# One Trainium2 core, a two-layer block with attention, convolution and linear attention: taps and low parts of weights get tied places in VectorE's queue

## The chip, the core and the metric

The kernel runs on one core of one Trainium2 chip. Its engines work beside each other, each through its own queue in the order in which the program was written to it: TensorE (PE) multiplies matrices, VectorE (DVE), ScalarE (ACT) and GpSimd (POOL) work on tiles, SyncE (SP) starts DMAs. An instruction at the head of a queue that waits for another engine holds up all that stand behind it. Times are device microseconds (us); the measured time of a kernel is the median of several runs.

## The reference

A token stream of 1024 channels goes through two layers of a first block and two more of a second. Each layer of the first block has a mixer with three branches over the same normalised and modulated input: attention with 8 heads (2 for keys and values) and rotary positions, gated linear attention (GLA), and a convolution. The convolution is the part that matters here:

```
glu   = a * sigmoid(g)                       # 1024 channels, from two projections of 1024 columns
conv  = depthwise_conv(glu, w_dw, width 31)  # 31 taps per channel, along the tokens
u     = layernorm(conv) * gain + bias
out_c = silu(u) @ w_conv_o                   # 1024 x 1024
f     = sum over branches of gate_b * (branch_b @ w_b)
```

All of it is in fp32. After the mixer comes a gated feed-forward network.

## The kernel before

**Products in three parts.** An fp32 product is computed as three products of rounded parts. A weight tile of 128 columns and 1024 rows (`raw`, 1 MB by DMA for two tiles) is split by `wsplit` (line 354 and on): ScalarE rounds it to the high part (`whi`, line 362), DVE subtracts to get the low part (`wlo`, listed under line 288, as every two-input operation is). For each of the eight blocks of 128 rows `mm_fm` (lines 386 to 388) then issues hi x hi, hi x lo and lo x hi, 24 matmuls in all; for keys, values and queries (lines 467 to 469) weights and data change sides. There are two `raw` buffers, three of `whi`, three of `wlo`, and three PSUM buffers `pm` for the results, which ScalarE or DVE must empty before they are used again.

**Two mixers.** In the first layer a mixer works on 512 tokens (512 columns per matmul), in the second on 256. The first takes the time from about 60 to 600 us, the second from about 1200 to 1700 us.

**Convolution.** `conv` computes 30 taps per channel tile on DVE as scalar_tensor_tensor instructions, acc = glu * w + acc, and the middle one with the bias on ScalarE. It does two channel tiles at a time (`ca_10457` and `ca_10458` are the first two of the second mixer, `ca_10463` and `ca_10464` the last); after a pair, GpSimd adds it to the channel sum `cs`. `conv_taps` loads the tap weights (`cwr`), transposes them on TensorE (line 1310) and copies them out as `cw`. `conv_norm` multiplies the finished sum by a constant matrix (`ones_d`, line 1346) to spread the mean over the partitions, subtracts it, squares, sums the squares (`csq`, `onesk`, line 1366), takes the rstd on GpSimd, scales and splits the result in parts for the product with `w_conv_o`.

**What sets the order.** The Python program is a set of generators, called lanes. Projections go along the main line, and at every projected tile `tick` lets each lane advance by its rate: the lane "conv" by CRATE0 = 1.3 steps in the first mixer and CRATE1 = 1.0 in the second, where a step is two taps of two channel tiles, so four DVE instructions. `merge` projects the gates (`mt`, a tanh on ScalarE) of a branch and its output product; before the latter, `flush` runs the lanes that the branch needs to their end. A scheduler then puts the recorded instructions into the queues by priority, with times of its own; taps carry priority 600 (CP), `wsplit` a more urgent one (WP = -100). `issue_after` gives it an extra edge: the instruction may not stand ahead of the one named. On one and the same engine that needs no semaphore.

Of the kernel before, what the change touches and what calls it, by code (L numbers as in the profile page):

```python
# [9 lines left out]
F32 = mybir.dt.float32  # L10
# [3 lines left out]
ALU = mybir.AluOpType  # L14
# [8 lines left out]
          "g": 5664, "gate": 6688}  # L23
WP = -100
CRATE0 = 1.3
CRATE1 = 1.0
ARATE0 = 0.6
ARATE1 = 0.6
GRATE0 = 0.8
GRATE1 = 0.6  # L30
CP = 600
PLO0A = 0
PLO0B = 0
PLO0 = PLO0A, PLO0B
PLO1A = 0
# [136 lines left out]
class Act:  # L172
    def __init__(self, hi, lo, hp=None, lp=None):
        self.hi, self.lo, self.hp, self.lp = hi, lo, hp, lp
# [13 lines left out]
class Builder:  # L188
    NU = 71

    def __init__(self, ctx, tc, ins, out, dbg=None, stop=None):
        self.tc, self.nc, self.I, self.out = tc, tc.nc, ins, out
        self.dbg, self.stop = dbg, stop
        self.n = 0
        self.lanes = {}
        self.pool_lo = 0
        self.nsplit = 0
        self.wpri = WP
        self.behind = None
        self.fheld = None  # L200
        self.spare = {}
        self.lo_behind = []
        self.hook = self.lo_after = None
        self.ns = [None]
        P = lambda **k: ctx.enter_context(tc.tile_pool(**k))
        self.cp = P(name="cp", bufs=1)
        self.sp = P(name="sp", bufs=12)
        self.up = P(name="up", bufs=self.NU)
        self.wp = P(name="wp", bufs=2)
        self.rp = P(name="rp", bufs=2)  # L210
        self.hp = P(name="hp", bufs=3)
        self.lp = P(name="lp", bufs=3)
        self.pm = P(name="pm", bufs=3, space=PSUM)
        self.ps = P(name="ps", bufs=5, space=PSUM)
# [63 lines left out]
        for _ in gen:  # L278
            pass

    def flush(self, *lanes):
        ls = [self.lanes[k] for k in lanes if k in self.lanes]
        while any(l[0] for l in ls):
            for l in ls:
                self.step(l)

    def tt(self, out, a, b, op, eng=None):
        return (eng or self.nc.vector).tensor_tensor(out=out, in0=a, in1=b, op=op)  # L288
# [68 lines left out]
    def wsplit(self, src, shape, pri=None):  # L357
        hi = self.hp.tile(list(shape), F32R, tag="whi", name=self.nm("whi"))
        lo = self.lp.tile(list(shape), F32R, tag="wlo", name=self.nm("wlo"))
        self.nsplit += 1  # L360
        with self.pri(self.wpri if pri is None else pri):
            self.nc.scalar.copy(hi, src)  # L362
            on_pool = self.pool_lo and self.nsplit % self.pool_lo == 0
            after = self.lo_behind.pop() if self.lo_behind else None
            with self.tc.issue_after(after.ins) if after else nullcontext():
                self.tt(lo, src, hi.bitcast(F32), ALU.subtract, self.nc.gpsimd if on_pool else None)
        return hi, lo

    def fm(self, w, c0, ncols, nk=8):
# [945 lines left out]
    def conv(self, l, cts, glu, acc, csum, cw, ns):  # L1315

        v = lambda x: x.rearrange("p (s t) -> p s t", s=ns)
        with self.pri(CP):
            for c in cts:
                self.act(acc[c], glu[c], AF.Identity, scale=cw[:, c, 15:16], bias=self.vt0[:, 8 * l + c : 8 * l + c + 1])  # L1320
        n = 0
        for k in range(31):
            d = k - 15
            if d == 0:
                continue
            lo, hi = max(0, -d), 256 - max(0, d)
            with self.pri(CP):
                for c in cts:
                    a = v(acc[c])[:, :, lo:hi]
                    self.stt(a, v(glu[c])[:, :, lo + d : hi + d], cw[:, c, k : k + 1], a, ALU.mult, ALU.add)  # L1330
            n += 1
            if n == 30:
                with self.pri(CP):
                    if cts[0] == 0:
                        self.tt(csum, acc[0], acc[1], ALU.add, self.nc.gpsimd)
                    else:
                        for c in cts:
                            self.tt(csum, csum, acc[c], ALU.add, self.nc.gpsimd)
            if n % 2 == 0:
                yield  # L1340
# [126 lines left out]
    def mixer(self, l, a, xs, start):  # L1467
# [9 lines left out]
        glu, acc = [], [self.u((128, T), F32, "ca") for _ in range(8)]  # L1477
# [9 lines left out]
        for m in range(0, 8, 2):  # L1487
# [13 lines left out]
            if m == 0:  # L1501
                cw = self.conv_taps(l)
            self.bg("conv", [self.conv(l, (m, m + 1), glu, acc, csum, cw, len(xs))], (CRATE0, CRATE1)[l])
        self.run(ai), self.run(gi)
        self.flush("mod")
        self.rope_tabs(l)
        kn, v = {}, {s: [self.u((128, 2, 256), F32R, n) for n in ("vh", "vl")] for s in both}
# [50 lines left out]
        def merge(bi, wname, oact, pre=0, lanes=(), then=None):  # L1558

            gi = self.proj_fm(w, IN_OFF["gate"] + bi * D, D, ar, T)  # L1560
            gts = []

            def gate():
                t = self.uh(T, "mt")
                self.act(t, next(gi), AF.Tanh, scale=0.5)
                gts.append(t)

            for _ in range(pre):
                gate()
            self.flush(*lanes)  # L1570
            if callable(oact):
                oact = oact()
            if then:
                then()
            yi = self.proj_fm(I[wname][l], 0, D, oact, T)
            for m in range(8):
                if m >= pre and m % 2 == 0:
                    gate(), gate()
                t, py = gts[m], next(yi)
                self.stt(t, t, 1.0, py, ALU.add, ALU.mult)  # L1580
                if macc[m] is None:
                    macc[m] = t
                else:
                    self.tt(macc[m], macc[m], t, ALU.add, nc.gpsimd if MP >> (2 * l + bi % 2) & 1 else None)
            self.run(gi), self.run(yi)
# [12 lines left out]
        if VG[l]:  # L1598
            vproj()
        merge(0, "w_att_o", oatt, PRE0[l], ("heads", "att"), None if GLE[l] else logs)  # L1600
        oatt = kT = qT = None
        self.flush("gla", "conv")

        self.pool_lo = (PLO0, PLO1)[l][1]
        ocv = self.act_alloc(8, T)
# [2 lines left out]
        self.bg("gla", [self.gla_scores(xs, kg, qg, A)], (GRATE0, GRATE1)[l] * len(xs))  # L1608
        acc = glu = csum = None
        merge(2, "w_conv_o", ocv, PRE2[l], ("conv",))  # L1610
        ocv = None
        if not VG[l]:
# [71 lines left out]
        elif PH1:  # L1684
            self.bg("pre", [self.prehold([(I["w_out"][l], 0, 512, 512)], PW1)])
        merge(1, "w_gla_o", gated, PRE1[l], ("gla",))
        rs = rp = on = og = kg = qg = vg = A = None
        self.B = self.st = None
# [491 lines left out]
```

## Time and profile before

| | |
|---|---|
| median of 3 runs | 2551.83 us (2550.2 to 2553.7) |
| the profiled execution | 2553.78 us, its span 2551.9 us |
| mean granted clock of TensorE | 0.98 |
| PE busy | 2418.1 us, 95% of the span |
| DVE busy | 1624.0 us, 64% |
| ACT busy | 1180.8 us, 46% |
| POOL busy | 518.1 us, 20% |
| DMA | 345.41 MB, 135 GB/s |

Busy times are shares of the whole span; what an engine is worth in a stretch is read from that stretch alone. The matmuls of 256 columns start 0.12 us apart at full clock, those of 512 columns 0.23 us. In the lists of waits and the timelines a bracket holds the idle time of the engine ahead of an instruction, and what ended it.

### The profile page before, as it was taken

What the parts mean: (1) busy time and instruction counts of PE and PEld (TensorE: products, weight loads), DVE (VectorE), ACT (ScalarE), POOL (GpSimd) and SP (SyncE); (2) the same over time, 40 slices, a digit from 0 to 9 for tenths busy, and PEclk for the clock granted to TensorE, in tenths of its full rate; (3) what the DMA queues carried; (4) which work ended last, traced back from release to release, by engine and by line L of the source; (5) the groups of instructions that cost most, each with busy time, mean ns of one, the idle gap of its engine ahead of it and who ended that gap; (6) DMA issues with size and microseconds to landing.
All of it is one profiled execution on the core that took longest, in us unless ns stands there. A gap on an engine that the chain in (4) does not pass through costs nothing. (4 is left out here: it accounts for less than half of the span.)

```text
span 2551.9 us, 38718 instructions
## 1 busy us (share of the span) xinstructions
PE 2418.1 (95%) x15227; PEld 2079.3 (81%) x15227; DVE 1624.0 (64%) x2700; ACT 1180.8 (46%) x2225; POOL 518.1 (20%) x460
## 2 busy tenths in 40 slices
PE   7989999899999999999899997998999999999998
PEld 5767887688877777776879897888987899888997
DVE  5878997884365443343799687766625656556564
ACT  3224567654343322232445855653443644446443
POOL 1002003791014000003310006531062100112001
PEclk9999999999999999999999998999999999999999
DMA  8432203223433444355233242642664246643454
GB/s 254 150 129 78 83 21 99 67 84 108 140 100 132 143 158 162 116 187 189 73 124 100 85 150 84 198 149 87 218 206 134 92 157 211 199 145 106 155 192 149
DMA packets 277690, 345.41 MB, mean 135 GB/s; under 512 B 12894, under 2 KB 208888, under 8 KB 277508
## 3 DMA queue, kind: packets, MB, share of 16 engines
q1 hardware_dynamic: 277508, 342.94, 41.7%
q8 instruction: 120, 1.97, 0.3%
q14 instruction: 62, 0.51, 0.1%
HBM read 341.85 MB, written 1.05 MB: 134 GB/s over the span
## 5 line engine op out<-in xcount | busy, mean ns | idle before, releaser
L386 PE MATMUL pm<-hi,whi 128*128 128x256 f32 (+1 forms) x2824 | 918.6, 327 | 23.5 <-ACT mt L298 13.1
L387 PE MATMUL pm<-lo,whi 128*128 128x256 f32 (+1 forms) x2824 | 911.4, 323 | 3.5 <-POOL lo L288 2.0
L388 PE MATMUL pm<-hi,wlo 128*128 128x256 f32 (+1 forms) x2824 | 909.5, 323 | 5.2 <-DVE wlo L288 5.1
L362 ACT CAST whi<-raw 128x1024 fp32r<-128x1024 f32 (+1 forms) x464 | 484.1, 1048 | 838.1 <-PE pm L387 506.2
L288 DVE TENSOR_TENSOR wlo<-raw,whi 128x1024 fp32r<-128x1024 f32 (+2 forms) x437 | 551.6, 1265 | 410.6 <-ACT whi L362 409.2
L386 PEld LDWEIGHTS pm<-hi,whi 128*128 128x128 f32 x2824 | 541.2, 192 | 68.2 <-ACT mt L298 13.9
L387 PEld LDWEIGHTS pm<-lo,whi 128*128 128x128 f32 x2824 | 542.7, 192 | 50.5 <-issue 7.4
L388 PEld LDWEIGHTS pm<-hi,wlo 128*128 128x128 f32 x2824 | 541.8, 192 | 46.5 <-DVE wlo L288 7.2
L291 DVE SCALAR_TENSOR_TENSOR ca<-gt,cw,ca 128x242 f32<-128x242 f32 (+28 forms) x480 | 267.6, 607 | 0.2
L468 PE MATMUL pm<-wlo,hi 128*128 128x512 f32 x536 | 211.8, 395 | 9.3 <-DVE wlo L288 7.1
L467 PE MATMUL pm<-whi,hi 128*128 128x512 f32 x536 | 213.4, 398 | 5.5 <-DVE qn L288 5.5
L469 PE MATMUL pm<-whi,lo 128*128 128x512 f32 x536 | 211.0, 394 | 0.0
L288 POOL TENSOR_TENSOR s<-s,mhalf 128x1 f32<-128x1 f32 (+2 forms) x82 | 67.0, 816 | 483.7 <-DVE s L295 445.1
L288 POOL TENSOR_TENSOR hl<-hr,hh 128x512 fp32r<-128x512 f32 (+1 forms) x38 | 56.6, 1492 | 472.7 <-ACT hh L454 416.9
L468 PEld LDWEIGHTS pm<-wlo,hi 128*128 128x128 f32 x536 | 101.9, 190 | 32.5 <-DVE wlo L288 7.5
L467 PEld LDWEIGHTS pm<-whi,hi 128*128 128x128 f32 x536 | 101.9, 190 | 29.1 <-issue 4.7
L469 PEld LDWEIGHTS pm<-whi,lo 128*128 128x128 f32 x536 | 101.6, 190 | 21.4
L288 POOL TENSOR_TENSOR eq<-B 128x256 f32<-128x256 f32 x96 | 91.3, 971 | 51.0 <-DVE ptot L291 27.7
L288 POOL TENSOR_TENSOR ek<-B 128x256 f32<-128x256 f32 (+1 forms) x100 | 100.1, 1020 | 1.1 <-DVE mt L288 0.6
L288 POOL TENSOR_TENSOR wlo<-raw,whi 128x1024 fp32r<-128x1024 f32 (+1 forms) x35 | 80.6, 2316 | 95.2 <-ACT whi L362 89.8
L467 PE MATMUL pm<-hh,hi 128*128 128x512 f32 (+2 forms) x258 | 92.6, 362 | 4.9 <-ACT hh L432 2.5
L468 PE MATMUL pm<-hl,hi 128*128 128x512 f32 (+2 forms) x258 | 93.0, 362 | 1.3 <-POOL hl L288 1.0
(327 smaller groups left out, 3362.3 us busy)
## 6 DMA issues: line engine op xcount, KB each, us to landing
raw<-in_w_in_dram SPq DMA_DIRECT2D x84, 1024.0 KB
aw<-in_w_ada_dram SPq DMA_DIRECT2D x192, 256.0 KB
raw<-in_w_gate_up_dram SPq DMA_DIRECT2D x40, 1024.0 KB
raw<-in_w_ff_gate_dram SPq DMA_DIRECT2D x21, 1024.0 KB
raw<-in_w_ff_up_dram SPq DMA_DIRECT2D x21, 1024.0 KB
raw<-in_w_down_dram SPq DMA_DIRECT2D x20, 1024.0 KB
raw<-in_w_ff_down_dram SPq DMA_DIRECT2D x18, 1024.0 KB
raw<-in_w_att_o_dram SPq DMA_DIRECT2D x8, 1024.0 KB
```

The lines of the kernel that those rows point to most:

```text
L288: return (eng or self.nc.vector).tensor_tensor(out=out, in0=a, in1=b, op=op)
L291: return self.nc.vector.scalar_tensor_tensor(out=out, in0=a, scalar=s, in1=b, op0=op0, op1=op1)
L362: self.nc.scalar.copy(hi, src)
L386: mm(out, lhsT=hi[:, k, :], rhs=a.hi[k], start=(first and k == 0), stop=False)
L387: mm(out, lhsT=hi[:, k, :], rhs=a.lo[k], start=False, stop=False)
L388: mm(out, lhsT=lo[:, k, :], rhs=a.hi[k], start=False, stop=(last and k == nk - 1))
L467: f(p, lhsT=a.hi[kk][:, sl], rhs=hi, start=first, stop=False)
L468: f(p, lhsT=a.hi[kk][:, sl], rhs=lo, start=False, stop=False)
L469: return f(p, lhsT=a.lo[kk][:, sl], rhs=hi, start=False, stop=last)
```

## The change

The lane "conv" advances by 1.2 steps per tile in the second mixer. Each conv step leaves its last tap in a list (`taps`), and `wsplit` remembers the last low part that DVE makes (`last_lo`). A low part is then ordered behind the third last step recorded (CLAG = 3), and every tap behind the last low part recorded. In the first `merge` of a mixer, `flush` advances the lane "conv" by two steps per round beside the attention lanes. After the flush of "gla" and "conv" the list is emptied. The number of instructions on PE, DVE, POOL and SP is the same as before. In the rows of order below, line numbers after the change are 10 to 16 higher for the same line of code.

```diff
-CRATE1 = 1.0
+CRATE1 = 1.2
+FRATE = 2.0
+CLAG = 3
...
-    def flush(self, *lanes):
+    def flush(self, *lanes, along=None, rate=1.0):
+
         ls = [self.lanes[k] for k in lanes if k in self.lanes]
+        al, n = self.lanes.get(along), 0.0
         while any(l[0] for l in ls):
             for l in ls:
                 self.step(l)
+            n += rate
+            while al and n >= 1.0:
+                n -= 1.0
+                self.step(al)
...
             after = self.lo_behind.pop() if self.lo_behind else None
+            if len(self.taps) >= CLAG:
+                after = self.taps[-CLAG]
             with self.tc.issue_after(after.ins) if after else nullcontext():
-                self.tt(lo, src, hi.bitcast(F32), ALU.subtract, self.nc.gpsimd if on_pool else None)
+                i = self.tt(lo, src, hi.bitcast(F32), ALU.subtract, self.nc.gpsimd if on_pool else None)
+                if not on_pool:
+                    self.last_lo = i
...
-            with self.pri(CP):
+            with self.pri(CP), self.tc.issue_after(self.last_lo.ins) if self.last_lo else nullcontext():
                 for c in cts:
                     a = v(acc[c])[:, :, lo:hi]
-                    self.stt(a, v(glu[c])[:, :, lo + d : hi + d], cw[:, c, k : k + 1], a, ALU.mult, ALU.add)
+                    i = self.stt(a, v(glu[c])[:, :, lo + d : hi + d], cw[:, c, k : k + 1], a, ALU.mult, ALU.add)
             n += 1
+            if n % 2 == 0:
+                self.taps.append(i)
...
-            self.flush(*lanes)
+            self.flush(*lanes, along="conv" if bi == 0 else None, rate=FRATE)
...
         self.flush("gla", "conv")
+        self.taps = []
```

On DVE in the first mixer, between the first and the second pair of channel tiles (`ca_127` and `ca_128`, then `ca_129` and `ca_130`): `wlo_1268` is the low part of the first K/V weight tile, `adar_1225` the sum of modulation and bias that needs eight matmuls of TensorE and a copy on ScalarE. Before:

```order
151 L291 SCALAR_TENSOR_TENSOR ca_128<-gt_661,cw_677,ca_128 128x2x241
152 L288 TENSOR_TENSOR wlo_1268<-raw_1265,whi_1267 128x1024
153 L288 TENSOR_TENSOR wlo_1300<-raw_1265,whi_1299 128x1024
154 L291 SCALAR_TENSOR_TENSOR gt_1152<-gt_1152,ga_1041 128x512
155 L295 TENSOR_SCALAR modT<-ps_1192 128x8
156 L288 TENSOR_TENSOR wlo_1334<-raw_1331,whi_1333 128x1024
157 L291 SCALAR_TENSOR_TENSOR gt_1189<-gt_1189,ga_1078 128x512
158 L288 TENSOR_TENSOR adar_1225<-adar_1225,ab_1198 4x512
159 L291 SCALAR_TENSOR_TENSOR ca_129<-gt_818,cw_677,ca_129 128x2x241
160 L291 SCALAR_TENSOR_TENSOR ca_130<-gt_858,cw_677,ca_130 128x2x241
```

After:

```order
154 L301 SCALAR_TENSOR_TENSOR gt_1189<-gt_1189,ga_1078 128x512
155 L305 TENSOR_SCALAR modT<-ps_1463 128x8
156 L298 TENSOR_TENSOR adar_1225<-adar_1225,ab_1198 4x512
157 L301 SCALAR_TENSOR_TENSOR ca_129<-gt_818,cw_677,ca_129 128x2x241
158 L301 SCALAR_TENSOR_TENSOR ca_130<-gt_858,cw_677,ca_130 128x2x241
159 L301 SCALAR_TENSOR_TENSOR ca_129<-gt_818,cw_677,ca_129 128x2x242
160 L301 SCALAR_TENSOR_TENSOR ca_130<-gt_858,cw_677,ca_130 128x2x242
161 L298 TENSOR_TENSOR wlo_1268<-raw_1265,whi_1267 128x1024
```

The low part, which stood six rows ahead of the modulation's sum, now stands behind it and behind the first four taps of the next pair. On TensorE the modulation's eight matmuls moved ahead of the K/V tile's, and on SP their weight loads ahead of a `raw` load.

On DVE at the start of the second mixer, where the tap weights are copied out (`cw_10624`), `gt` is the glu that the taps read and `wlo_10727` and `wlo_10785` are the low parts of the next two gate and value tiles. Before:

```order
1184 L288 TENSOR_TENSOR wlo_10727<-raw_10724,whi_10726 128x1024
1185 L288 TENSOR_TENSOR wlo_10785<-raw_10724,whi_10784 128x1024
1186 L291 SCALAR_TENSOR_TENSOR gt_10608<-gt_10608,ga_10499 128x256
1187 L691 BN_AGGR mv_10673<-bn_10670 128x2
1188 L295 TENSOR_SCALAR s_10675<-mv_10673 128x1
1189 L291 SCALAR_TENSOR_TENSOR s_10681<-mv_10673,s_10677 128x1
1190 L288 TENSOR_TENSOR wlo_10843<-raw_10840,whi_10842 128x1024
1191 L295 TENSOR_SCALAR cw_10624<-ps_10615 128x248
1192 L288 TENSOR_TENSOR wlo_10880<-raw_10840,whi_10879 128x1024
```

After:

```order
1187 L301 SCALAR_TENSOR_TENSOR gt_10608<-gt_10608,ga_10499 128x256
1188 L305 TENSOR_SCALAR cw_10624<-ps_10615 128x248
1189 L301 SCALAR_TENSOR_TENSOR ca_10457<-gt_10561,cw_10624,ca_10457 128x241
1190 L301 SCALAR_TENSOR_TENSOR ca_10457<-gt_10561,cw_10624,ca_10457 128x242
1191 L301 SCALAR_TENSOR_TENSOR ca_10458<-gt_10608,cw_10624,ca_10458 128x241
1192 L301 SCALAR_TENSOR_TENSOR ca_10457<-gt_10561,cw_10624,ca_10457 128x243
1193 L301 SCALAR_TENSOR_TENSOR ca_10458<-gt_10608,cw_10624,ca_10458 128x242
1194 L298 TENSOR_TENSOR wlo_10727<-raw_10724,whi_10726 128x1024
1195 L301 SCALAR_TENSOR_TENSOR ca_10458<-gt_10608,cw_10624,ca_10458 128x243
1196 L301 SCALAR_TENSOR_TENSOR ca_10457<-gt_10561,cw_10624,ca_10457 128x244
1197 L301 SCALAR_TENSOR_TENSOR ca_10458<-gt_10608,cw_10624,ca_10458 128x244
1198 L298 TENSOR_TENSOR wlo_10785<-raw_10724,whi_10784 128x1024
```

The two low parts stood ahead of the copy of the tap weights; now they stand behind it and behind five and eight taps of the first pair.

On TensorE at the end of the second mixer's convolution, `ps_13658` is the product of the channel sum `cs` with `ones_d`, and `pm` are gate tiles of the convolution's branch. Before:

```order
7027 L388 MATMUL pm_13871<-hi_10007,wlo_13868 128x256
7028 L386 MATMUL pm_13871<-hi_10008,whi_13867 128x256
7029 L387 MATMUL pm_13871<-lo_10012,whi_13867 128x256
7030 L1346 MATMUL ps_13658<-cs_10465,ones_d 128x256
7031 L388 MATMUL pm_13871<-hi_10008,wlo_13868 128x256
7032 L386 MATMUL pm_13871<-hi_10008,whi_13867 128x256
```

After:

```order
6947 L400 MATMUL pm_13632<-hi_10010,whi_13628 128x256
6948 L401 MATMUL pm_13632<-lo_10014,whi_13628 128x256
6949 L402 MATMUL pm_13632<-hi_10010,wlo_13629 128x256
6950 L1362 MATMUL ps_13658<-cs_10465,ones_d 128x256
6951 L400 MATMUL pm_13686<-hi_10007,whi_13682 128x256
6952 L401 MATMUL pm_13686<-lo_10011,whi_13682 128x256
6953 L402 MATMUL pm_13686<-hi_10007,wlo_13683 128x256
```

The product stood eight matmuls into the tile `pm_13871`; now it stands three tiles and these eight matmuls earlier, right behind `pm_13632`. On DVE the last taps of `ca_10463` and `ca_10464` moved with it, from ahead of `wlo_13973`, which is for a tile behind `pm_13871`, to ahead of `wlo_13434`, twelve low parts earlier.

## Rows read from the trace of the kernel before

**Rows 1.** The page, busy time, share of the span and instructions of each engine
```profile
PE 2418.1 (95%) x15227; PEld 2079.3 (81%) x15227; DVE 1624.0 (64%) x2700; ACT 1180.8 (46%) x2225; POOL 518.1 (20%) x460
```
**Rows 2.** Stretches: length, busy PE, PEld, DVE, ACT, POOL, clock, DMA share, GB/s
```profile
130.00:200.00 70.00, 60.67 (x273) 46.88 (x272) 51.47 (x93) 21.27 (x68) 7.26 (x6) 0.90 0.38 128
...
1250.00:1310.00 60.00, 55.03 (x363) 51.23 (x362) 52.27 (x103) 30.52 (x51) 12.61 (x11) 0.91 0.48 149
...
1440.00:1500.00 60.00, 58.01 (x389) 53.30 (x389) 37.72 (x75) 51.41 (x72) 0.00 (x0) 1.00 0.33 103
...
1520.00:1567.00 47.00, 31.82 (x203) 30.68 (x202) 39.13 (x68) 25.75 (x57) 22.18 (x26) 0.78 0.36 112
```
**Rows 3.** Waits of PE, 1500 to 1570 us: total us, times, longest
```profile
PE pm L386 <- ACT mt L298: 12.0, 2, 6.7
PE ps L1346 <- POOL cs L288: 3.2, 1, 3.2
```
**Rows 4.** Timeline of PE, 1519 to 1567: start, us, instruction, [idle before <- releaser]
```profile
1519.91 0.28 PE L386 MATMUL pm<-hi,whi 128*128 128x256 f32 x1
...
1532.89 1.22 PE L1346 MATMUL ps<-cs,ones_d 128*128 128x256 f32 x2 [3.23 <-POOL cs L288]
...
1534.13 0.41 PE L386 MATMUL pm<-hi,whi 128*128 128x256 f32 x1
1534.34 0.41 PE L387 MATMUL pm<-lo,whi 128*128 128x256 f32 x1
...
1543.94 1.28 PE L1366 MATMUL ps<-onesk,csq 128*128 128x1 f32 x5
...
1566.43 0.41 PE L386 MATMUL pm<-hi,whi 128*128 128x256 f32 x1
```
**Rows 5.** Timeline of POOL, the end of the channel sum
```profile
1531.24 1.60 POOL L288 TENSOR_TENSOR cs<-cs,ca 128x256 f32<-128x256 f32 x2 [105.73 <-DVE ca L291]
```
**Rows 6.** Timeline of ACT, the mt of the second stop
```profile
1560.72 0.36 ACT L298 ACTIVATE mt<-pm 128x256 f32<-128x256 f32 x1
```
**Rows 7.** Timeline of DVE, 1440 to 1500 us, low parts and taps
```profile
1461.78 1.23 DVE L288 TENSOR_TENSOR wlo<-raw,whi 128x1024 fp32r<-128x1024 f32 x1 [5.25 <-ACT whi L362]
...
1487.21 0.97 DVE L291 SCALAR_TENSOR_TENSOR ca<-gt,cw,ca 128x241 f32<-128x241 f32 x2
...
1496.03 2.01 DVE L291 SCALAR_TENSOR_TENSOR ca<-gt,cw,ca 128x246 f32<-128x246 f32 x5
```
**Rows 8.** Timeline of PE in the first mixer, 133 to 190 us
```profile
133.11 0.40 PE L468 MATMUL pm<-wlo,hi 128*128 128x512 f32 x1
...
188.52 0.80 PE L468 MATMUL pm<-wlo,hi 128*128 128x512 f32 x1 [7.12 <-DVE wlo L288]
189.11 0.63 PE L469 MATMUL pm<-whi,lo 128*128 128x512 f32 x1
189.54 0.63 PE L467 MATMUL pm<-whi,hi 128*128 128x512 f32 x1
```
**Rows 9.** Timeline of DVE in the first mixer, 122 to 180 us
```profile
122.16 2.12 DVE L288 TENSOR_TENSOR wlo<-raw,whi 128x1024 fp32r<-128x1024 f32 x1 [0.49 <-ACT whi L362]
...
145.46 0.68 DVE L288 TENSOR_TENSOR adar<-adar,ab 4x512 f32<-4x512 f32 x1 [10.59 <-ACT adar L638]
...
179.41 6.02 DVE L291 SCALAR_TENSOR_TENSOR ca<-gt,cw,ca 128x508 f32<-128x508 f32 x9
```
**Rows 10.** Waits of PE, 125 to 250 us
```profile
PE ps L915 <- DVE ra L288: 3.2, 1, 3.2
```
**Rows 11.** Timelines of PE and DVE at the start of the second mixer
```profile
1256.64 0.40 PE L1310 MATMUL ps<-cst,cwr 31*128 31x31 f32 x4 [1.59 <-DMA cwr<-in_conv_w_dw_dram]
...
1259.42 0.58 PE L1310 MATMUL ps<-cst,cwr 31*128 31x31 f32 x4 [1.53 <-DMA cwr<-in_conv_w_dw_dram]
...
1263.54 0.58 PE L386 MATMUL pm<-hi,whi 128*128 128x256 f32 x1 [1.53 <-ACT ga L1491]
...
1260.03 0.42 DVE L295 TENSOR_SCALAR cw<-ps 128x248 f32<-128x248 f32 x1 [3.40 <-PE ps L1310]
```

More of the change, by code (lines that the diff above doesn't have):

```diff
@@ L202, in __init__ @@
         self.lo_behind = []
+        self.last_lo = None
+        self.taps = []
         self.hook = self.lo_after = None
@@ L1602, in mixer @@
         self.flush("gla", "conv")
+        self.taps = []
         self.pool_lo = (PLO0, PLO1)[l][1]
```

## The prediction

> **What bounds the kernel now.** I read the page's busy times first. TensorE is busy for 2418 of 2552 us [rows 1], so a change of order can gain only from its 134 us of gaps and from the stretches in which its clock is halved, and can lose wherever it makes TensorE wait. Next I cut the first block's two mixers into stretches [rows 2]. Almost all of TensorE's loss in them lies in three: 130 to 200 us (60.7 us busy of 70, clock 0.90), 1250 to 1310 (55.0 of 60, clock 0.91) and 1520 to 1567 (31.8 of 47, clock 0.78). In the last one the list of waits has three entries that matter, 12.0 us in two waits for ScalarE's mt and 3.2 us for GpSimd's cs [rows 3]. The timelines of the single engines then say why.
>
> **The end of the second mixer's convolution.** The reader is to follow one chain. DVE has little to do ahead of 1487 us: before the low part at 1461.8 it stands still for 5.3 us until ScalarE has made the high part [rows 7], and in 1440 to 1500 it is busy for 37.7 of 60 us [rows 2]. Only at 1487.2 does it begin the taps of the last pair of channel tiles (ca_10463 and ca_10464 in the order) [rows 7]. So GpSimd's channel sum waits until 1531.2 for those taps [rows 5], and TensorE, which has the ones_d product of that sum in its queue, stops at 1529.7 until 1532.9 [rows 3, 4]. Then the chain of the normalisation (subtract, square, sum, rstd, scale, split) runs with hardly any matmuls left to stand beside it: TensorE stops for 6.7 and for 5.3 us more [rows 3], both times for a PSUM buffer that ScalarE has not yet emptied, since its mt, at 1560.7 the second time [rows 6], stands in ScalarE's queue behind pieces of this chain.
>
> **The change part by part.** No operation is added or taken away; what moves is order, and with the low parts the release of weight buffers. The 240 taps of a layer cost what they did: 0.40 us each in the second mixer (five in 2.01 us) beside 1.2 us for a low part [rows 7].
>
> First, the end of the second mixer. With 1.2 steps per tile and the two kinds of DVE work tied together, the last pair's taps stand between the low parts of the tiles of 1455 to 1500. 60 taps of 0.40 us are 24 us. Some 18 of them were in that stretch already (1487 to 1500), the other 42 need 17 us, and DVE had 22.3 us free there [rows 2]. So they should end about 1500 instead of 1531, with each low part some 2 to 3 us ahead of its first matmul; I price this at 0 to +2 us and take 0. What this gives is in the order of TensorE: ones_d now stands one matmul after the eighth gate tile, ahead of the matmul that starts at 1519.9 [rows 4], and the sum it needs is then 20 us old. From there to the second tile after the chain (1566.4) the kernel takes 46.5 us [rows 4]. In it are seven tiles of 24 matmuls at 0.12 us, 20.2 us, and some 2 us of small ones; 24 us are waits and half clock. In the new order the chain starts 13 us earlier and has 61 tile matmuls (7.3 us) between ones_d and the sums of squares, where it takes 11.0 us now (1532.9 to 1543.9, [rows 4]): about 3 us of wait remain there. From the sums to the mt that holds up the next-to-last tile it takes 16.8 us now (1543.9 to 1560.7, [rows 4, 6]), against 12 us of tile and small matmuls: 3.5 us of wait, and about 2 more at the rstd and at the split parts. With 4 us of half clock that is 12.5 of the 24, so 12 us are saved. Bounds: 18 us if the clock stays up and the chain is shorter in emptier queues, 6 us if the waits add up as they stand now.
>
> After such a stop the rows show matmuls of 256 columns 0.21 us apart instead of 0.12: 1534.1 and on, after a wait of 3.2 us [rows 4]. Of 512 columns they go at 0.43 instead of 0.23 after the wait of 7.1 [rows 8], a granted clock at the lower of two levels, 1.2 instead of 2.4 GHz. The Trainium skill (TensorE: Matmul & The Clock Gate, Part 1: The HAM clock gate) says that the slow state is the default and that activity releases it, and so speaks against a change that turns three long stops into four short ones. If by that rule each of the four cost a half-clock stretch like the one after 1532.9, the gain here would fall to about 9 us; if none did, it would be near 16. No row of this stretch shows four such stops in a row.
>
> Second, the first mixer, 130 to 200 us. Taken away is the longest wait there: TensorE stands from 181.4 to 188.5 for a low part that DVE computes only after eleven taps and an add, and then runs 14 matmuls at half clock, 14 x 0.20 = 2.8 us [rows 8, 9]. Now DVE has that low part every four taps, and its sum of durations puts it at about 185, when TensorE, late by the next paragraph, comes for it. So some 10 us go.
>
> Added is a wait at 133 us. There TensorE's first K/V matmul with a low part starts at 133.1 [rows 8], on a low part that DVE made from 122.2 to 124.3, ready with 9 us to spare [rows 9]. In the new order this one (wlo_1268) stands behind the add of adar and four taps of the next pair, and the adar behind eight matmuls of the modulation, which TensorE now does before the K/V tiles. In the rows of before the adar add starts at 145.5 after 10.6 us idle [rows 9]. Moved up with its matmuls, it can start at about 134.5; four taps of 0.64 and the low part of 1.2 bring the low part to 138 to 141, and TensorE to a stop of 4 to 6 us, with 2 us of half clock. Behind it on DVE stand the next low parts and the K norms, so that the wait for the first qn at 160 grows by about 1. Together 5 + 2 + 1 = +8, and −10 + 8 = −2. In 220 to 245 DVE is then further ahead with its taps than before, and the wait for ra there (3.2 us [rows 10]) may shrink: I take −1 more, in all −3, between −9 (the new stop is 2 us and that wait goes too) and +6 (the new stop is 10 us and the old one only moves).
>
> Third, the start of the second mixer, 1250 to 1310 us. TensorE's eight transposes of the tap weights (cwr) wait for their DMA at 1256.6 and 1259.4 in either order [rows 11]. Now they stand before 22 matmuls that before filled the time around them, and wlo_10727 stands behind the weights' copy and five taps, so those matmuls can't start until the copy at 1260.0 [rows 11], two first terms on ScalarE (1 us), five taps (2.0) and the low part (1.2): about 1264.4. The 44 matmuls of two tiles, the first half of them at half clock, take 22 x 0.21 + 22 x 0.12 = 7.3 us and end near 1271.7. In the order of before, 24 of them and 9 transposes are left at 1263.5, after the last of three stops [rows 11]: 33 x 0.21 = 6.9 us, 1270.4. That is +1. For the next 40 us DVE needs 1.2 + 4 to 6 x 0.40 = 2.8 to 3.6 us per weight tile and TensorE 24 x 0.12 = 2.9, so TensorE is pushed back by up to 2 us, most of which later stops give back, where TensorE waits for norms that DVE makes no later than before. I take +1.5; from −2 to +20 (a rival, below).
>
> The remaining places I cost at nothing: ahead of 130 us in the first mixer four to eight taps (2.6 to 5 us) now stand before each low part, and the cover is a lead like the 9 us above; where it is gone, a low part that is late costs the duration of a tap or two, 0.6 to 1.3 us. In the later parts the same DVE work fits between the same matmuls.
>
> **The sum.** −12 − 3 + 1.5 = −13.5 us. The profiled execution took 2553.8 us (span 2551.9 and 1.9 around it), 2 us above the median of 2551.8. On the median this gives 2538 us.
>
> **The rivals.**
> The first: DVE becomes the bound of the second mixer's first stretch. For it speaks that DVE is already busy for 52.3 of the 60 us after 1250 [rows 2]. If it has six taps at every one of the next 20 tiles, it falls behind TensorE by 3.6 − 2.9 = 0.7 us at each, 14 us, and with half clock after the stops 20 us. It decides once the lag is over 15 us, because then the gains of the other two places are eaten: 2553.8 + 20 − 12 − 3 is 2559, on the median 2557. Against it: the order has four taps between most low parts, not six, and in the attention part much of DVE's work waits for TensorE and ScalarE and not the reverse.
> The second: the end of the convolution is early but the chain stays as long as it is, because ScalarE and GpSimd work through the gated linear attention's pieces in the same queues; the waits for mt stay at two thirds. Then 6 of the 12 us come: 2544.
> The third: ties hold DVE back more than forecast in the first mixer (+6 instead of −3) and the end brings 8: 2551.8 − 8 + 6 + 1.5 = 2551, no change that can be seen.
> The fourth: all the stops shrink, −18 − 7 − 1 = −26: 2526.
>
> **How the numbers follow.** Forecast and its neighbourhood (2532 to 2542): 0.40. Second rival: 0.20. Fourth: 0.13. Third: 0.13. First: 0.14. A difference of 0.2% (5.1 us) is about what a measurement of this kernel can tell from none. Faster by more is the forecast, the second and the fourth, less a little of the second's edge: 0.71. Same: 0.14. Slower: 0.15. The range 2527 to 2556 leaves out the outer half of the fourth and of the first. The likeliest case's own range is 2532 to 2544.
>
> **What would show it.** Right: the ones_d product runs at 1510 to 1525 without a wait, and no wait for mt there is over 4 us; the stretch corresponding to 1520 to 1567 takes some 34 us; the wait at 181 is gone and one of 4 to 6 us stands near 135; in 1250 to 1265 TensorE stops about 10 us in all. Wrong: low parts named as what TensorE waits for over 1264 to 1345 or 1480 to 1500 with more than 5 us in all, or a stop for mt of 5 us or more beside a ones_d product that was on time.

## The result, and the profile after

The changed kernel takes 2567.9 us (median of 4 runs, 2564.7 to 2571.5) against 2552.5 us before in the same sessions: ratio 1.0062, 95% interval 1.0044 to 1.0079. It is 15 us slower, where 14 us faster was forecast. The profiled execution took 2568.5 us, its span is 2566.7 us.

The page of the changed kernel, part 1, answers to [rows 1]: the engines' busy times are the same within 8 us. The counts are equal but for two more table loads on ScalarE (27 against 25).

```profile
PE 2425.9 (95%) x15227; PEld 2082.4 (81%) x15227; DVE 1623.2 (63%) x2700; ACT 1183.6 (46%) x2227; POOL 517.8 (20%) x460
```

Where the time went is seen by laying the two traces on each other by the number of the matmul: both have 15227 of them, and the order of most is the same. The table has the start of the n-th matmul, and how much later than before it comes in the changed kernel and in the kernels of the experiments below, e1 to e8 in their order (us).

```
matmul  before   after   e1    e2    e3    e4    e5    e6    e7    e8    what lies ahead of it
  600    127.9   -0.8  -1.4  -0.5  -0.6  -0.5  -0.3  -1.4  -0.5  -0.3
 1250    281.4    3.8  -1.6   6.6  -0.7   4.0  -0.3  -1.7  -0.7  -0.5  first mixer, keys, values, queries
 2250    468.4    7.5  -2.8   3.3  -0.7   0.8  -0.4  -1.7  -0.3  -0.5  first mixer, attention
 6550   1248.6    9.1  -2.8   3.1  -0.2   1.9  -0.1  -1.5   2.3  -0.6
 6650   1269.2    9.4  -2.5   4.0  -0.2   2.3   0.0  -1.2   2.5  -0.3  second mixer, tap weights
 7250   1372.3   25.4  -2.4   8.7  16.0  18.4  16.6  -1.0  -0.2   0.9  second mixer, keys, values, queries
 8300   1523.7   26.9   0.8  15.1  17.7  20.1  19.0   1.8   2.0   1.5  second mixer, attention and gates
 8550   1573.5   12.6 -13.5  11.6   3.3   5.7   4.3 -12.5 -13.8 -10.2  end of the convolution
 8850   1599.8   15.7 -11.5  11.6   6.3   8.7   7.4 -10.5 -10.9  -5.9  just behind it
```

Read as differences between neighbouring rows: the changed kernel loses 8.3 us in the first mixer (from −0.8 to 7.5), almost nothing at the tap weights (0.3), 16.0 us in the keys, values and queries of the second mixer, gains 14.3 us at the end of its convolution and gives 3.1 back right behind it. From matmul 8850 on it stays some 15 us late. Each column is one execution; the kernels whose first mixer is that of before (e1, e3, e5, e7, e8) take 153.2 to 153.4 us from 600 to 1250 and 185.8 to 187.4 from 1250 to 2250, so differences of about 2 us in a long stretch say little.

The stretches of the changed kernel, columns as in [rows 2]; the last one holds the end of the convolution, and the second and third the stretch that lost most:

```profile
130.00:205.00 75.00, 63.63 (x293) 47.65 (x292) 62.74 (x111) 21.47 (x68) 8.15 (x7) 0.93 0.27 86
...
1272.00:1330.00 58.00, 50.65 (x327) 45.91 (x326) 55.62 (x107) 25.07 (x43) 9.27 (x9) 0.97 0.43 134
1330.00:1395.00 65.00, 54.07 (x297) 45.06 (x297) 57.61 (x124) 27.02 (x81) 9.13 (x10) 0.92 0.27 83
...
1547.00:1580.00 33.00, 27.92 (x204) 27.20 (x203) 28.51 (x48) 24.56 (x56) 17.66 (x22) 0.90 0.34 107
```

DVE is busy for 55.6 of 58 us and TensorE for only 50.7 in the second row: the roles have changed. The last stretch shows the gain: 33 us at clock 0.90 for the work that took 47 at 0.78 in [rows 2].

The waits of TensorE from 1255 to 1395 us in the changed kernel:

```profile
PE pm L482 <- DVE wlo L298: 7.1, 3, 3.4
PE pm L402 <- DVE wlo L298: 4.9, 3, 2.2
PE ps L929 <- DVE ra L298: 4.2, 4, 2.1
PE ps L1324 <- DMA cwr<-in_conv_w_dw_dram: 4.0, 2, 3.2
PE pm L400 <- ACT ga L1507: 2.6, 2, 1.9
```

Twelve us are waits for low parts, none of which stood in the list before but for 0.3 us. Those in the first mixer, 125 to 250 us, answer to [rows 8] and [rows 10]:

```profile
PE pm L482 <- DVE wlo L298: 9.1, 3, 4.9
PE pm L402 <- DVE wlo L298: 3.2, 2, 2.4
PE pm L481 <- DVE qn L298: 2.2, 4, 0.9
PE pm L400 <- ACT whi L372: 1.2, 1, 1.2
PE ps L929 <- DVE ra L298: 0.5, 1, 0.5
```

And around the end of the second mixer's convolution, 1500 to 1605 us, they answer to [rows 3]:

```profile
PE pm L400 <- ACT mt L308: 4.1, 2, 3.3
PE pm L402 <- DVE wlo L298: 3.6, 3, 2.0
PE pm L400 <- ACT whi L372: 2.3, 1, 2.3
PE ps L1310 <- POOL s L298: 1.1, 1, 1.1
PE ps L1382 <- DVE csq L298: 0.5, 1, 0.5
```

The waits for mt fall from 12.0 to 4.1 us, and that for cs is gone.

How DVE became the bound is seen in the count of taps. Laid between the same two matmuls, 6550 and 7250, the tile view of `ca` has 112 taps before and 140 after (the first line is the kernel before, the second the changed one; count, then shortest, median and longest in ns, first and last start).

```profile
L291 DVE SCALAR_TENSOR_TENSOR ca<-gt,cw,ca x112: 457/471/956, 1263.4 to 1370.0; 128x245 f32<-128x245 f32 x8, 128x246 f32<-128x246 f32 x8, 128x247 f32<-128x247 f32 x8, 128x248 f32<-128x248 f32 x8
```

```profile
L301 DVE SCALAR_TENSOR_TENSOR ca<-gt,cw,ca x140: 455/471/951, 1270.1 to 1397.4; 128x241 f32<-128x241 f32 x10, 128x242 f32<-128x242 f32 x10, 128x243 f32<-128x243 f32 x10, 128x244 f32<-128x244 f32 x10
```

The same stretch as a whole, in the kernel before and then in the changed one:

```profile
1248.60:1372.30 123.70, 111.81 (x703) 100.78 (x703) 109.52 (x225) 60.15 (x136) 20.99 (x19) 0.94 0.41 126
```

```profile
1257.70:1397.70 140.00, 115.83 (x703) 101.08 (x702) 121.42 (x253) 61.32 (x139) 19.50 (x21) 0.93 0.35 106
```

DVE does 28 instructions more, all of them taps, and is busy 11.9 us longer; TensorE takes 16.3 us longer for the same 700 matmuls (140.0 against 123.7). These taps were worth nothing there: before, DVE did them after 1372, where it had time.

What DVE waited for in this stretch, in the kernel before (1250 to 1370 us) and then in the changed one (1255 to 1395):

```profile
DVE qn L288 <- POOL s L288: 6.0, 8, 0.9
DVE wlo L288 <- ACT whi L362: 3.4, 3, 1.8
DVE cw L295 <- PE ps L1310: 3.4, 1, 3.4
DVE s L291 <- POOL s L288: 0.7, 1, 0.7
DVE hTl L288 <- ACT hTh L302: 0.3, 1, 0.3
```

```profile
DVE qn L298 <- POOL s L298: 7.1, 8, 1.8
DVE cw L305 <- PE ps L1324: 6.6, 1, 6.6
DVE gt L301 <- ACT gt L308: 2.9, 3, 1.4
DVE s L301 <- POOL s L298: 0.7, 1, 0.7
DVE ca L301 <- ACT ca L308: 0.7, 1, 0.7
```

The 14.2 us in which DVE was not busy before (123.7 less 109.5) did not take the taps up: 13.8 of them are these waits in its own queue, and of these only the 3.4 us for whi went, while others grew and came. In the changed kernel they are 18.0 of 18.6 us. So 11.9 us of work came on top of the idle time, and 4.4 us more of idle time with it: together the 16.3.

### The profile page after: what moved, and what is told of

Its sections match the earlier page's. It is cut to its first block, busy times and chain, and to the rows that moved or that the text cites. A ratio compares the mean times of both kernels' runs of the same rounds, so it can differ in the third digit from the quotient of the medians.

```text
span 2566.7 us, 38721 instructions
## 1 busy us (share of the span) xinstructions
PE 2425.9 (95%) x15227; PEld 2082.4 (81%) x15227; DVE 1623.2 (63%) x2700; ACT 1183.6 (46%) x2227; POOL 517.8 (20%) x460
## 5 line engine op out<-in xcount | busy, mean ns | idle before, releaser
L301 DVE SCALAR_TENSOR_TENSOR ca<-gt,cw,ca 128x242 f32<-128x242 f32 (+29 forms) x480 | 268.1, 610 | 6.8 <-ACT ca L308 6.6
L482 PE MATMUL pm<-wlo,hi 128*128 128x512 f32 x536 | 213.8, 399 | 18.4 <-DVE wlo L298 16.2
L298 POOL TENSOR_TENSOR ek<-B 128x256 f32<-128x256 f32 (+1 forms) x100 | 93.8, 956 | 2.4 <-PE ps L1220 1.8
```

The source lines that it names most:

```text
L301: return self.nc.vector.scalar_tensor_tensor(out=out, in0=a, scalar=s, in1=b, op0=op0, op1=op1)
L482: f(p, lhsT=a.hi[kk][:, sl], rhs=lo, start=False, stop=False)
```

## The experiments

Ratios are to the kernel before, with 95% intervals. The working theory was: the ties of low parts to taps bring taps into stretches where DVE has no time, and the higher rate alone earns what the end gains. Its rivals: the rate does the harm; the taps' tie does; or waiting, not DVE's time, is what counts.

**The rate alone (e1).**

```diff
 (the kernel before)
-CRATE1 = 1.0
+CRATE1 = 1.2
```

> The kernel before with the second mixer's rate at 1.2 and nothing else: no ties, no conv steps beside the attention flush. In the order the last pair's taps end 14 low parts earlier than before and the ones_d product stands at the same place as in the changed kernel, while pairs one to three end where they did before. Theory (the ties cost, the rate gains): about 2552.5 - 14 at the end of the second mixer + 3 given back right after = 2541 us, and 1250 to 1395 us runs as before. Rival (the higher rate itself crowds DVE in 1280 to 1395): that stretch loses its 17 us here too, 2557 to 2559 us. Second rival (the end's gain needs the ties, since without them low parts come late behind taps in 1440 to 1500): 2550 to 2555 us.

Measured: 2542.7 us, ratio 0.9968 (0.9955 to 0.9980), as the theory had it. From 6550 to 7250 it takes 124.1 us, as before (123.7); at the end it gains 14.3, after a loss of 3.2 from 7250 to 8300, where the taps now stand. The sum of the channels is ready at 1492 us, and DVE's idle time from 1452 to 1475 is full of taps:

```profile
1451.48 1.20 DVE L298 TENSOR_TENSOR wlo<-raw,whi 128x1024 fp32r<-128x1024 f32 x1
1452.60 4.32 DVE L301 SCALAR_TENSOR_TENSOR ca<-gt,cw,ca 128x243 f32<-128x243 f32 x11
1456.84 1.22 DVE L298 TENSOR_TENSOR wlo<-raw,whi 128x1024 fp32r<-128x1024 f32 x1
...
1459.90 5.18 DVE L301 SCALAR_TENSOR_TENSOR ca<-gt,cw,ca 128x249 f32<-128x249 f32 x13
1464.99 1.22 DVE L298 TENSOR_TENSOR wlo<-raw,whi 128x1024 fp32r<-128x1024 f32 x1
1466.13 5.19 DVE L301 SCALAR_TENSOR_TENSOR ca<-gt,cw,ca 128x255 f32<-128x255 f32 x13
```

GpSimd's last additions of that kernel's channel sum, against [rows 5]:

```profile
1490.75 1.63 POOL L298 TENSOR_TENSOR cs<-cs,ca 128x256 f32<-128x256 f32 x2 [68.04 <-DVE ca L301]
```

The two rivals, harm from the rate and a gain that needs the ties, are out.

**The ties alone (e2).**

```diff
 (the changed kernel)
-CRATE1 = 1.2
+CRATE1 = 1.0
...
-            self.flush(*lanes, along="conv" if bi == 0 else None, rate=FRATE)
+            self.flush(*lanes, along=None, rate=FRATE)
```

> The changed kernel with the second mixer's rate back at 1.0 and without conv steps beside the attention flush: only the ties are left. Theory (ties make DVE the bound at the start of each mixer): the first mixer loses 4 to 8 us, 1250 to 1395 us loses 10 to 17 us, the end of the convolution gains at most 3: 2565 to 2575 us. Rival (the rate is what loses in the second mixer): only the first mixer's loss stays, 2552.5 + 4 to 8 - 3 = 2554 to 2558 us.

Measured: 2563.5 us, 1.0043 (1.0028 to 1.0058), slower; the rival is out. The sum is near the theory's, its parts are not: 3.8 us are lost in the first mixer (−0.5 to 3.3), 5.6 from 6550 to 7250, not 10 to 17, and 6.4 more up to 8300; 3.5 are gained at the end. So the loss of 16 us at keys, values and queries needs both, ties and rate.

**Ties in the second mixer only (e3).**

```diff
 (the changed kernel)
-            if n % 2 == 0:
+            if n % 2 == 0 and l == 1:
                 self.taps.append(i)
...
-            with self.pri(CP), self.tc.issue_after(self.last_lo.ins) if self.last_lo else nullcontext():
+            with self.pri(CP), self.tc.issue_after(self.last_lo.ins) if self.last_lo and l == 1 else nullcontext():
...
-            self.flush(*lanes, along="conv" if bi == 0 else None, rate=FRATE)
+            self.flush(*lanes, along=None, rate=FRATE)
```

> The changed kernel with ties in the second mixer alone and no conv steps beside the attention flush, rate 1.2. Theory: the first mixer's 7.5 us come back and nothing else: 2567.9 - 7.5 = 2560 us, 1250 to 1395 us still 17 us longer than before. Rival (the second mixer's loss comes from what the first one handed over, later weights or buffers): that loss shrinks too, below 2552 us.

Measured: 2562.2 us, 1.0037 (1.0024 to 1.0050). The first mixer is as before, the second loses 16.2 us from 6550 to 7250 as in the changed kernel: it hands nothing over. It is 2.2 us above the theory's 2560.

**No steps beside the attention flush (e4).**

```diff
 (the changed kernel)
-            self.flush(*lanes, along="conv" if bi == 0 else None, rate=FRATE)
+            self.flush(*lanes, along=None, rate=FRATE)
```

> The changed kernel without the conv steps beside the attention flush; ties and rate stay. In the order only the first mixer's last pair moves, to 7 low parts later. Theory: the loss of 3.7 us at 335 to 360 us (TensorE waits for ScalarE's PT there) goes, and the later taps make GpSimd's channel sum up to 4 us later at 450: 2564 to 2568 us. Rival (those waits come from the ties): 2568 to 2572 us.

Measured: 2564.1 us, 1.0048 (1.0033 to 1.0062). At matmul 1250 it is as late as the changed kernel (4.0 against 3.8), at 2250 it is 0.8 against 7.5. So with this lag the steps beside the flush cost the attention of the first mixer up to 6.7 us; the medians differ by 3.8. They don't cost it by themselves: the kernel with a lag of six (e9, below) keeps them, and from 1250 to 2250 it takes 185.2 us, 187.0 before. Why the lag matters there was not tried. In the changed kernel TensorE waits there for ScalarE's PT, from 345 to 362 us (from 250 to 460 us the kernel before has 2.7 us of such waits):

```profile
PE ps L1009 <- ACT PT L312: 4.4, 4, 2.0
```

**One direction of the ties at a time (e5, e6).** First the low parts' tie, with the second mixer's edits as above; the taps' tie is taken out:

```diff
 (as "ties in the second mixer only")
-            with self.pri(CP), self.tc.issue_after(self.last_lo.ins) if self.last_lo and l == 1 else nullcontext():
+            with self.pri(CP):
```

> The second mixer's ties in one direction only, rate 1.2, no conv steps beside the attention flush: each low part stays behind the third last conv step, taps are free. Theory (the low part's tie makes TensorE wait for taps): 1250 to 1395 us loses about as much as with both ties, 16 us, and the end gains 14: 2558 to 2563 us. Rival (taps held behind low parts push the norms and rope back): the stretch loses at most 3 us, 2540 to 2546 us.

Measured: 2561.6 us, 1.0036 (1.0023 to 1.0049), 16.7 us lost from 6550 to 7250, as with both (16.2 in e3). Then the taps' tie:

```diff
 (as "no steps beside the attention flush")
-            if len(self.taps) >= CLAG:
-                after = self.taps[-CLAG]
```

> The other direction alone, in both mixers: each tap behind the last low part recorded, low parts free, rate 1.2, no conv steps beside the attention flush. Theory: nothing is lost in either mixer's start (within 2 us of before), the end gains as with the rate alone: 2540 to 2545 us. Rival (this tie is what costs): first mixer +4 to 8, second +10 or more, 2555 us or more.

Measured: 2541.9 us, 0.9956 (0.9939 to 0.9973). Neither mixer's start loses. So it is the edge that holds a low part, which TensorE waits for, behind taps, which nobody waits for yet.

**Shorter taps in a similar order (e7).**

```diff
 (as "ties in the second mixer only")
             lo, hi = max(0, -d), 256 - max(0, d)
+            if l == 1 and cts[0] < 6:
+                hi = lo + 64
```

> As the kernel with both ties in the second mixer alone and rate 1.2 (2562 us), but the taps of the second mixer's first three pairs work on 64 columns instead of some 250, so about 0.2 us less each; 180 taps. What they leave out is part of the convolution. The queues' order is nearly that of that kernel. Theory (DVE's time is the bound between 1275 and 1395): with some 30 us less of work there the waits for low parts go and the stretch loses at most 4 us against before, 2545 to 2550 us. Rival (a low part waits because taps wait for ScalarE and GpSimd, not because they take long): the stretch still loses over 10 us, 2556 us or more.

Measured: 2539.9 us, 0.9949 (0.9934 to 0.9965), below what the theory had. The stretch from 6550 to 7250 takes 121.1 us instead of 139.8, with DVE busy for 97.0 of them instead of 121.3. Here are this kernel's stretch and that of the kernel with full taps:

```profile
1251.00:1372.10 121.10, 109.44 (x702) 98.17 (x702) 96.99 (x260) 60.71 (x137) 20.50 (x21) 0.96 0.42 128
```

```profile
1248.50:1388.30 139.80, 116.02 (x702) 101.27 (x701) 121.33 (x253) 61.30 (x139) 19.55 (x21) 0.93 0.35 106
```

It has not fewer DVE instructions but shorter ones, and TensorE's waits for low parts fall from 12.0 to 1.3 us. The order on DVE is not quite the same, but no lighter: counted from matmul 6550, 54 taps stand ahead of the tenth low part, 48 with full taps, 34 before. So what the taps take of DVE's time is the cause, not that taps wait for other engines.

**A higher rate (e8).** As the first experiment with CRATE1 = 1.4.

> The kernel before with the second mixer's rate at 1.4, no ties. In the order the last pair's taps end six low parts earlier than at 1.2, while the ones_d product stands at the same place. Theory (at 1.2 the channel sum is already 20 us old when TensorE comes to it): no further gain at the end, and 0 to 4 us lost or won at 1440 to 1500 where taps stand denser: 2539 to 2547 us. Rival (denser taps make low parts late in 1300 to 1420): 2548 us or more.

Measured: 2548.9 us, 0.9984 (0.9975 to 0.9993). The theory's time was off; the rival's was met, but not by its mechanism: the start loses little (1.5 us from 6550 to 7250). The end gains 11.7 us, less than at rate 1.2, with waits for the sums of squares of 2.9 us against 0.7, and 4.3 go again just behind it, against 2.0, with a wait for a high part of 4.9 us against 2.3. Why these waits are longer was not tried.

**A longer lag (e9, e10).** The changed kernel with CLAG = 6, then 10.

> The changed kernel, everything in it, but a low part is tied behind the sixth last conv step instead of the third last. In the order the second mixer's first two pairs end two and three low parts later than with a lag of three, still one and two earlier than before. Theory (the fewer taps a low part has to wait for, the less DVE is the bound at 1275 to 1395): half of the changed kernel's loss there remains, 2548 to 2557 us. Rival (any tie of a low part to a recent tap costs as much): 2562 us or more.

> As the last one with a lag of ten steps. In the order all pairs but the last end at the same low part as before, the last one as in the changed kernel. Theory: no loss in either mixer's start, the end gains as with the rate alone: 2540 to 2546 us. Rival (the ties still reorder the norms and the rope in between): 2552 us or more.

Measured: 2549.3 us, 0.9984 (0.9973 to 0.9995), and 2544.1 us, 0.9971 (0.9961 to 0.9980). Both as the theory had it: the further a low part's tie lies back in the taps, the less is lost, and at ten steps it no longer costs. With lag 6 the waits for low parts between 1250 and 1395 us are down to one line:

```profile
PE pm L482 <- DVE wlo L298: 4.9, 3, 3.2
```

**Both in one (e11).** In the profiled execution with lag 6 the first mixer gained some 3 us. So its ties and flush steps were kept in the first mixer alone, with the rate 1.2 and no ties in the second:

```diff
 (the changed kernel)
-CLAG = 3
+CLAG = 6
...
-            if n % 2 == 0:
+            if n % 2 == 0 and l == 0:
                 self.taps.append(i)
...
-            with self.pri(CP), self.tc.issue_after(self.last_lo.ins) if self.last_lo else nullcontext():
+            with self.pri(CP), self.tc.issue_after(self.last_lo.ins) if self.last_lo and l == 0 else nullcontext():
...
-            self.flush(*lanes, along="conv" if bi == 0 else None, rate=FRATE)
+            self.flush(*lanes, along="conv" if bi == 0 and l == 0 else None, rate=FRATE)
```

> The ties of the changed kernel with a lag of six steps, and the conv steps beside the attention flush, in the first mixer alone; the second mixer has no ties and the rate 1.2. Theory (with lag six the first mixer gained some 3 us and the second lost 9 before its end; the rate alone loses nothing there): the rate's gain and 3 us more, 2536 to 2541 us. Rival (the 3 us were chance of one profiled execution): as with the rate alone, 2541 to 2544 us.

Measured: 2543.7 us, 0.9963 (0.9949 to 0.9977): the rival. The fastest forms, the rate alone (0.9968), the rate with the taps' tie (0.9956) and this one, can't be told apart; all beat both kernels by about 10 and 25 us. The rate alone is the smallest edit, one number.

## Why the prediction was wrong

**The end of the second mixer's convolution** was right in mechanism: −12 forecast, −14.3 measured at matmul 8550. The ones_d product ran at 1546.7 us without a wait, the sum being ready 20 us before:

```profile
1523.53 2.71 POOL L298 TENSOR_TENSOR cs<-cs,ca 128x256 f32<-128x256 f32 x2 [85.36 <-DVE ca L301]
```

```profile
1546.65 0.59 PE L1362 MATMUL ps<-cs,ones_d 128*128 128x256 f32 x2
```

Of the waits forecast there (about 3 us at the sums of squares, about 2 at the rstd and the split parts, 3.5 for mt) the trace has 0.7, 1.1 and 3.3. The half clock cost about 3.3 us, an estimate from the granted clock of 0.90 over 33 us; 4 were forecast. That taps would fit between the low parts at no cost was nearly right: 1.4 us are lost from 7250 to 8100, where they stand. Not forecast was that 3.1 us are given back just behind, where TensorE waits for a high part and a low part (2.3 and 1.1 us at 1595) and its granted clock is 0.88 instead of 1.00. ScalarE makes that high part at 1594.1 us, behind eq and ek of the GLA branch, for which it waited 5.5 us for GpSimd between 1587 and 1594. That the −11.2 us left at matmul 8850 lie so near the −12 is in part luck: waits 3.4 us shorter than forecast and a loss behind them that was not seen.

**The first mixer** was wrong: +8.3 instead of −3. The added wait came as worked out: the adar add at 136.8 us, the low part done at 141.2, a stop of 4.9 us (4 to 6 forecast). DVE's timeline, then TensorE's:

```profile
136.81 0.68 DVE L298 TENSOR_TENSOR adar<-adar,ab 4x512 f32<-4x512 f32 x1 [0.27 <-ACT ca L308]
137.41 2.60 DVE L301 SCALAR_TENSOR_TENSOR ca<-gt,cw,ca 128x482 f32<-128x482 f32 x4
139.94 1.21 DVE L298 TENSOR_TENSOR wlo<-raw,whi 128x1024 fp32r<-128x1024 f32 x1
...
177.66 1.22 DVE L298 TENSOR_TENSOR wlo<-raw,whi 128x1024 fp32r<-128x1024 f32 x1
```

```profile
141.20 0.80 PE L482 MATMUL pm<-wlo,hi 128*128 128x512 f32 x1 [4.87 <-DVE wlo L298]
...
178.94 0.50 PE L482 MATMUL pm<-wlo,hi 128*128 128x512 f32 x1 [4.09 <-DVE wlo L298]
```

The step that failed is "Together 5 + 2 + 1 = +8, and −10 + 8 = −2". The low part ahead of the one that used to be late is now late itself, done at 178.9 us, and stops TensorE for 4.1 us; the wait moved by one weight tile, from 7.1 to 4.1 us, and was not taken away: the −10 was the term that failed. From 600 to 1250 DVE does 115 taps instead of 97 and is busy for 138.9 us instead of 126.9; with the taps' tie alone (e6) nothing is lost here, so it is the low parts' tie that costs. The prediction also read the old wait too lightly, as eleven taps and an add: the run of taps at 179.4 in [rows 9] is the rest of one of 20 that begins at 172.2. Further on, waits for low parts of 0.9 and 2.4 us replace the 3.2 us for ra. And the attention, costed "at nothing" because "the same DVE work fits between the same matmuls", lost 3.7 us: e4 shows that the steps beside the flush did it, with a lag of three.

**The start of the second mixer** decided. Up to matmul 6650 the forecast of +1 holds (0.3), though TensorE stops there for 5.9 us in all and not for about 10. The step that failed is "TensorE is pushed back by up to 2 us, most of which later stops give back". DVE's time per tile was set against TensorE's for the tiles of one kind only, taps at 0.40 us, and the sum over the whole stretch was not made: 28 taps more at 0.43 us are 11.9 us. By busy time alone they would still have fitted, 109.5 and 11.9 us into 123.7; but nearly all the rest were waits in DVE's own queue (13.8 us), and the taps did not fall into them: its idle time grew from 14.2 to 18.6 us. The sign that the prediction had named for being wrong, more than 5 us of waits for low parts, came: 12.0. That was the first rival, priced at +20 and given 0.14. Its mechanism is what happened and its price nearly so: 16.0 us; with the first mixer's 8.3 in place of −3 the kernel is 15 us slower.

The rival's counter-argument, that "the order has four taps between most low parts, not six", did not hold. Of the 27 low parts of that stretch 14 have four taps ahead of them and six have eight or nine; 140 taps to 27 low parts are 5.2 each, and it was 4.0 before. Beside GpSimd even four taps and a low part take longer than TensorE's tile, as the last section shows. And where DVE did wait for others, 7.1 us for GpSimd's s alone, this makes the lack greater and not smaller.

## What to carry to other kernels

If two streams on one engine are tied by an edge, tie the work nobody waits for behind the work that is waited for. In this kernel that direction cost nothing (e6) and the reverse cost 16.7 us in one stretch (e5), until the lag was so long that it cost nothing either (e10). Before moving work into a stretch, sum all of the engine's busy time in it, between two instructions that stay in place, and look at what its idle time there is: waits of its own queue take up new work only where that work is ready and stands ahead of them. Busy time alone would have passed this change (121.4 of 123.7 us), and a comparison per tile misses what the tiles of other kinds, the norms and the rope, take. An early start pays where an engine stands idle: here one number, the rate, filled 1452 to 1475 us, where DVE had waited for high parts, with taps and earned the whole gain.

## What the runs showed of the hardware

Taps that take 0.40 us each by themselves took 0.65 us beside GpSimd in the mean of four. In the changed kernel DVE's timeline has, beside GpSimd's four lo from 1279.9 to 1284.1 and from 1284.7 to 1289.2, and then without it:

```profile
1280.88 1.74 DVE L298 TENSOR_TENSOR wlo<-raw,whi 128x1024 fp32r<-128x1024 f32 x1
1282.55 2.60 DVE L301 SCALAR_TENSOR_TENSOR ca<-gt,cw,ca 128x249 f32<-128x249 f32 x4
...
1290.16 1.21 DVE L298 TENSOR_TENSOR wlo<-raw,whi 128x1024 fp32r<-128x1024 f32 x1
1291.29 1.65 DVE L301 SCALAR_TENSOR_TENSOR ca<-gt,cw,ca 128x253 f32<-128x253 f32 x4
```

GpSimd's timeline of the same kernel:

```profile
1279.85 4.24 POOL L298 TENSOR_TENSOR lo<-hf,hi 128x256 fp32r<-128x256 f32 x4 [18.70 <-ACT hi L308]
1284.72 4.46 POOL L298 TENSOR_TENSOR lo<-hf,hi 128x256 fp32r<-128x256 f32 x4 [0.63 <-ACT hi L308]
```

A low part grows from 1.21 to 1.74 us and four taps from 1.65 to 2.60: four taps and a low part are 4.3 us beside GpSimd, against the 2.9 that TensorE needs for a tile. Two of the waits for low parts, at 1282.7 and 1286.9 us, fall into this time. The growth is no factor: of the four taps, two take 0.95 us and two 0.47, and of the 140 in the stretch 134 take 0.46 to 0.48, five 0.95 and one 0.83. An instruction of DVE that was hit here grew by some 0.5 us, a tap as much as a low part. GpSimd's grow too: the two lo that lie beside the low parts took 1.54 and 1.71 us, the shortest lo of this kernel 0.72. This is not what the change added, though: the kernel before has five taps of 0.95 us there too, and only the two long low parts, 1.1 us in all, are new. The Trainium skill (SBUF — State Buffer, SBUF: two separate sides) says that DVE and GpSimd share a pair of ports and that whichever starts first holds it for its whole instruction, a DVE operation with two SBUF inputs against a GpSimd one that reads SBUF; these rows agree with it, as an instruction that is hit grows by a step and not in proportion to its length; no run here took GpSimd's work away to test it.
